# A 68-byte load on GpSimd, ahead of its constant fills, in an elementwise multiply-and-GELU kernel

## The chip, the core and the metric

The kernel runs on one core of one Trainium2 chip. The core has a vector engine (VectorE, DVE in the profile), a scalar engine (ScalarE, ACT), GpSimd (POOL), a tensor engine (PE, not used here) and SyncE (SP), which computes nothing and only waits and issues transfers. Transfers between the device memory and the core's on-chip memory (SBUF, 128 partitions) are carried out by 16 DMA engines that all issuing engines share. The metric is the device time of the program in microseconds, as the median of several executions.

## The reference

Two arrays of 1024 x 4096 float32 go in and one comes out. Each element is multiplied with its partner, and the product goes through the tanh form of GELU:

```python
z = x * y
return (0.5 * z * (1 + np.tanh(np.sqrt(2 / np.pi) * (z + 0.044715 * z ** 3)))).astype(np.float32)
```

There is no reuse of any element. 33.55 MB have to be read and 16.78 MB written.

## The kernel before

The 4,194,304 elements are seen as 128 partitions of 32,768 columns, cut into three pieces of columns: a small one of 1,280 columns (5 KB in each partition), one of 16,384 (64 KB) and one of 15,104 (59 KB). Each piece is contiguous in device memory, and within it each partition has one contiguous row. The buffer `xs` holds all of x on chip. The buffer `ys` holds only 20,440 columns, so the pieces of y share it: the 64 KB rows of y lie at columns 4,056 to 20,440 of `ys`, the 59 KB rows are written to columns 0 to 15,104 once VectorE has used the first part of the 64 KB rows, and the small piece comes last, to columns 15,104 to 16,384.

Six loads and three stores make up all the traffic. Two loads are issued ahead of everything: `_hoist` takes an issued instruction out of the place where it was written and puts it into the program's first block, ahead of that engine's first Drain, and so ahead of the barriers with which all engines start. SyncE so issues the small piece of x (`load_x(0)`, line 79), and ScalarE the 64 KB rows of x (`load_x(1)`, line 80). GpSimd in that first block fills four constants (memsets of one column each, put down to line 137) and then takes part in the start barriers. It does nothing after that.

The rest of the transfers is SyncE's queue, in this order: wait for the small piece of x (line 81), the 64 KB rows of y (line 82), the 59 KB rows of x (line 83), then, after VectorE's third multiply, the 59 KB rows of y, and after its fourth the small piece of y (lines 84 to 87). The stores follow (lines 112 to 116): the first one waits for the 59 KB rows of y to have landed and for ScalarE's fourth step, the others for ScalarE alone. Then SyncE waits for the stores, clears the semaphores and ends (lines 117 to 122).

VectorE multiplies in place (line 99) in 13 steps: four of 4,096 columns over the first pair of pieces, seven of 2,048 and one of 768 over the second, one of 1,280 over the last. ScalarE applies the GELU in place (line 107) to each step after VectorE. Semaphore `sem_mul` counts the multiplies, `sem_act` the activations, and each transfer has a semaphore of its own.

Of the kernel before, what the change touches and what calls it, by code (L numbers as in the profile page):

```python
# [1 line left out]

# [4 lines left out]


F32 = mybir.dt.float32
GELU = mybir.ActivationFunctionType.Gelu_apprx_tanh  # L10

PIECES = [(0, 1280), (1280, 17664), (17664, 32768)]

Y_LOADS = [(1280, 17664, 4056), (17664, 32768, 0), (0, 1280, 15104)]

Y_FREE = [0, 3, 4]

STEPS = [[4096] * 4, [2048] * 7 + [768], [1280]]  # L20
STORES = [(1280, 17664), (17664, 32768), (0, 1280)]
Y_BUF = 20440


def _hoist(nc, issued):

    here = nc.cur_bb.bb.instructions
    first = nc.main_func.blocks[0].instructions
    for ins in issued:
        del here[next(k for k, i in enumerate(here) if i is ins or i.name == ins.name)]  # L30
    engine = issued[0].engine
    at = next(
        k
        for k, i in enumerate(first)
        if i.engine == engine and type(i).__name__ == "InstDrain"
    )
    first[at:at] = issued


@with_exitstack  # L40
def kernel(
    ctx: ExitStack,
    tc: tile.TileContext,
    x: bass.AP,
    y: bass.AP,
    out: bass.AP,
):
    nc = tc.nc
    P = nc.NUM_PARTITIONS

    def columns(t, a, b):

        flat = t.flatten_outer_dims().rearrange("r c -> (r c)")
        pa, pb = next(q for q in PIECES if q[0] <= a and b <= q[1])
        return flat[P * pa : P * pb].rearrange("(p c) -> p c", p=P)[:, a - pa : b - pa]


    tc.close()
    tc.compile()

    xs = nc.alloc_sbuf_tensor("xs", [P, PIECES[-1][1]], F32).ap()
    ys = nc.alloc_sbuf_tensor("ys", [P, Y_BUF], F32).ap()
    sem_x = [nc.alloc_semaphore(f"sem_x{i}") for i in range(len(PIECES))]
    sem_y = [nc.alloc_semaphore(f"sem_y{i}") for i in range(len(Y_LOADS))]
    sem_mul = nc.alloc_semaphore("sem_mul")
    sem_act = nc.alloc_semaphore("sem_act")
    sem_o = [nc.alloc_semaphore(f"sem_o{i}") for i in range(len(STORES))]

    def load_x(i, engine=nc.sync):
        a, b = PIECES[i]  # L70
        return engine.dma_start(out=xs[:, a:b], in_=columns(x, a, b)).then_inc(sem_x[i], 16)

    def load_y(i):
        a, b, r = Y_LOADS[i]
        return nc.sync.dma_start(
            out=ys[:, r : r + b - a], in_=columns(y, a, b)
        ).then_inc(sem_y[i], 16)

    _hoist(nc, [load_x(0).ins])
    _hoist(nc, [load_x(1, nc.scalar).ins])  # L80
    nc.sync.wait_ge(sem_x[0], 16)
    load_y(0)
    load_x(2)
    for i in range(1, len(Y_LOADS)):
        if Y_FREE[i]:
            nc.sync.wait_ge(sem_mul, Y_FREE[i])
        load_y(i)

    nc.scalar.wait_ge(sem_x[0], 16)
    n = 0  # L90
    done = {}
    for i, (a, b, r) in enumerate(Y_LOADS):
        for j, (xa, xb) in enumerate(PIECES):
            if xa <= a < xb:
                nc.vector.wait_ge(sem_x[j], 16)
        nc.vector.wait_ge(sem_y[i], 16)  # L96
        c = a
        for w in STEPS[i]:
            nc.vector.tensor_mul(  # L99
                out=xs[:, c : c + w],  # L100
                in0=xs[:, c : c + w],
                in1=ys[:, r + c - a : r + c - a + w],
            ).then_inc(sem_mul, 1)
            n += 1
            done[c + w] = n
            nc.scalar.wait_ge(sem_mul, n)
            nc.scalar.activation(  # L107
                out=xs[:, c : c + w], in_=xs[:, c : c + w], func=GELU
            ).then_inc(sem_act, 1)
            c += w  # L110

    for i, (a, b) in enumerate(STORES):
        if i == 0:
            nc.sync.wait_ge(sem_y[-2], 16)
        nc.sync.wait_ge(sem_act, done[b])
        nc.sync.dma_start(out=columns(out, a, b), in_=xs[:, a:b]).then_inc(sem_o[i], 16)
    for i in range(len(STORES) - 1):
        nc.sync.wait_ge(sem_o[i], 16)
    nums = sorted(s.num for s in [*sem_x, *sem_y, *sem_o[:-1], sem_mul, sem_act])
    assert nums == list(range(nums[0], nums[-1] + 1))  # L120
    nc.sync.sem_clear(range(nums[0], nums[-1] + 1))
    nc.sync.wait_ge(sem_o[-1], 16).then_inc(sem_o[-1], -16)


# [1 line left out]
_INS = ['x', 'y']  # L126
_OUTS = [((1024, 4096), 'float32')]


# [23 lines left out]
```

## Time and profile before

| | value |
|---|---|
| median of 3 runs | 119.83 us (119.66 to 120.29) |
| profiled execution: span from the first instruction to the last | 118.5 us |
| profiled execution: a time of its own beside the span | none is given; the median of the runs is 1.3 us above the span |
| VectorE busy | 35.2 us (30%), 13 instructions |
| ScalarE busy | 30.9 us (26%), 14 instructions |
| GpSimd busy | 0.2 us, 4 instructions |
| bytes moved | 50.33 MB, 425 GB/s over the span |
| queue q1 (SyncE's transfers) | 41.94 MB |
| queue q10 (ScalarE's transfer) | 8.39 MB |

How to read it: instructions that only set registers, branch, wait, signal or issue a transfer are not counted as busy, so GpSimd's 0.2 us are its four constant fills alone. A row named SPq or ACTq is the issue of a transfer by SyncE or ScalarE; its duration is that of issuing, and the transfer's landing is given apart. The chain of work that ended last is followed back from the last instruction, and gives for each stretch what was being waited for.

### The profile page before, as it was taken

To read this page: it belongs to the slowest core of one execution; us is meant where nothing else is said; L and a number is where in the kernel's file an instruction comes from. 1 tells how busy PE (TensorE), PEld (TensorE's weight loads), DVE (VectorE), ACT (ScalarE), POOL (GpSimd) and SP (SyncE) were. 2 spreads that over 40 slices of the span, in tenths; PEclk is the share of its full clock that TensorE was granted. 3 is DMA by queue.
4 is the path that set the end of the run, shared out by engine and by line. 5 is a ranking of instruction groups with operands and counts; after the bars stand their busy time and mean duration, and the time that the engine had idled before them with its cause. 6 is when DMAs were issued, how large, how long until landed. Compare 5 with 4: busy or idle time off the path is not lost.

```text
span 118.5 us, 83 instructions
## 1 busy us (share of the span) xinstructions
DVE 35.2 (30%) x13; ACT 30.9 (26%) x14; POOL 0.2 (0%) x4
## 2 busy tenths in 40 slices
DVE  0000000000000069999920000059999940000000
ACT  0000000000000000999975000006998990000000
POOL 0000000000000000000000000000000000000000
DMA  9888899889988897798797797798899887977975
GB/s 492 382 382 382 354 597 464 354 354 465 597 354 354 354 632 347 326 632 347 326 632 347 326 632 347 326 575 354 354 531 531 354 354 326 653 326 326 653 326 221
DMA packets 1296, 50.33 MB, mean 425 GB/s; under 512 B 144, under 2 KB 144, under 8 KB 528
## 3 DMA queue, kind: packets, MB, share of 16 engines
q1 hardware_dynamic: 1152, 41.94, 82.3%
q10 hardware_dynamic: 144, 8.39, 16.5%
HBM read 33.55 MB, written 16.78 MB: 425 GB/s over the span
## 4 chain that ended last, share of the span: by engine, by line
DMA 55%; DVE 24%; ACT 3%; issue 1%; DVEq 0%
DMA ys<-in_y_dram 43%; DVE xs L99 24%; DMA xs<-in_x_dram 11%; ACT xs L107 3%; DVEq L96 0%
## 5 line engine op out<-in xcount | busy, mean ns | idle before, releaser
L99 DVE TENSOR_TENSOR xs<-xs,ys 128x2048 f32<-128x2048 f32 (+3 forms) x13 | 35.2, 2778 | 60.9 <-DMA ys<-in_y_dram 60.9
L107 ACT ACTIVATE xs<-xs 128x2048 f32<-128x2048 f32 (+3 forms) x13 | 29.6, 2300 | 19.6 <-DVE xs L99 19.6
L107 ACT ACT_TABLE_LOAD x1 | 1.3, 1283 | 47.2 <-DVE xs L99 47.2
L137 POOL MEMSET const-uint8-127<- 128x1 uint8 x1 | 0.1, 102 | 0.0
L137 POOL MEMSET const-bfloat16-1.0<- 128x1 bf16 x1 | 0.1, 101 | 0.0
L137 POOL MEMSET const-float32-0.0<- 128x1 f32 x1 | 0.1, 98 | 0.2 <-issue 0.2
L137 POOL MEMSET const-float32-1.0<- 128x1 f32 x1 | 0.1, 98 | 0.0
## 6 DMA issues: line engine op xcount, KB each, us to landing
xs<-in_x_dram SPq DMA_DIRECT2D x1, 7552.0 KB, 46.5
ys<-in_y_dram SPq DMA_DIRECT2D x1, 7552.0 KB, 22.5
out_dram<-xs SPq DMA_DIRECT2D x1, 7552.0 KB, 20.4
xs<-in_x_dram SPq DMA_DIRECT2D x1, 640.0 KB, 13.6
ys<-in_y_dram SPq DMA_DIRECT2D x1, 640.0 KB, 19.7
out_dram<-xs SPq DMA_DIRECT2D x1, 640.0 KB, 20.8
xs<-in_x_dram ACTq DMA_DIRECT2D x1, 30.4
ys<-in_y_dram SPq DMA_DIRECT2D x1, 29.0
```

The source lines that it names most:

```text
L99: nc.vector.tensor_mul(out=xs[:, c : c + w], in0=xs[:, c : c + w], in1=ys[:, r + c - a : r + c - a + w],).then_inc(sem_mul, 1)
L107: nc.scalar.activation(out=xs[:, c : c + w], in_=xs[:, c : c + w], func=GELU).then_inc(sem_act, 1)
L137: nc = _bacc.Bacc("TRN2", target_bir_lowering=False, num_devices=1)
```

## The change

GpSimd issues one more transfer: the first 17 elements of y (68 bytes, one contiguous stretch of the first row of its small piece) go to columns 0 to 17 of `ys` on partition 0. The data is not used: those columns are later overwritten by the 59 KB rows of y. The transfer signals a new semaphore, `sem_s`.

`_hoist` now also takes a Memset for the place to put an instruction in front of. SyncE's and ScalarE's hoisted loads stand where they stood, since those engines have no memset; GpSimd's new load comes ahead of its four constant fills, and is the first instruction of the kernel on that engine.

SyncE, ahead of the issue of y's 59 KB rows, waits for `sem_s` in addition to `sem_mul`, so that the 68 bytes can't land on top of them. The list of semaphores cleared at the end has one more in it. The order of all other instructions on every engine is as before.

```diff
+SPARE = 0
...
     at = next(
         k
         for k, i in enumerate(first)
-        if i.engine == engine and type(i).__name__ == "InstDrain"
+        if i.engine == engine and type(i).__name__ in ("InstDrain", "InstMemset")
     )
     first[at:at] = issued
...
+    sem_s = nc.alloc_semaphore("sem_s")
...
     _hoist(nc, [load_x(0).ins])
     _hoist(nc, [load_x(1, nc.scalar).ins])
+    spare = nc.gpsimd.dma_start(
+        out=ys[0:1, SPARE : SPARE + 17], in_=columns(y, 0, 17)[0:1, :]
+    ).then_inc(sem_s, 16)
+    _hoist(nc, [spare.ins])
     nc.sync.wait_ge(sem_x[0], 16)
     load_y(0)
     load_x(2)
     for i in range(1, len(Y_LOADS)):
         if Y_FREE[i]:
             nc.sync.wait_ge(sem_mul, Y_FREE[i])
+        if i == 1:
+            nc.sync.wait_ge(sem_s, 16)
         load_y(i)
...
-    nums = sorted(s.num for s in [*sem_x, *sem_y, *sem_o[:-1], sem_mul, sem_act])
+    nums = sorted(s.num for s in [*sem_x, *sem_y, *sem_o[:-1], sem_s, sem_mul, sem_act])
```

## The prediction

> **What bounds the kernel now.** I read the page first, then the chain of waits, then the timeline of the start, then what SyncE's queue waits for, and last a table of stretches.
>
> From the page, the engines, the traffic and the issues:
>
> ```profile
> span 118.5 us, 83 instructions
> DVE 35.2 (30%) x13; ACT 30.9 (26%) x14; POOL 0.2 (0%) x4
> ...
> HBM read 33.55 MB, written 16.78 MB: 425 GB/s over the span
> ...
> xs<-in_x_dram SPq DMA_DIRECT2D x1, 640.0 KB, 13.6
> ys<-in_y_dram SPq DMA_DIRECT2D x1, 640.0 KB, 19.7
> ```
>
> No engine is busy for a third of the span, and the DMA engines carry 425 GB/s from end to end. The last two lines are x's small piece, landing 13.6 us after its issue, and y's small piece, 19.7 us.
>
> The chain that ended last, in order of time, its first pieces:
>
> ```profile
> 0.00 13.56 DMA xs<-in_x_dram
> 13.56 0.02 issue
> 13.57 28.99 DMA ys<-in_y_dram
> ...
> 42.66 13.11 DVE xs L99 x3
> 55.77 0.02 issue
> 55.79 22.46 DMA ys<-in_y_dram
> ```
>
> The chain names VectorE between 42.66 and 55.77, but the transfers do not pause there, as the table of stretches below shows: x's 59 KB rows are still coming. So the bound is the byte count, and an instruction costs time only if it leaves the DMA engines without work.
>
> The timeline of the first 14 us (start, duration, what):
>
> ```profile
> 0.00 0.38 SPq L71 DMA_DIRECT2D xs<-in_x_dram  x1
> 0.12 0.36 ACTq L71 DMA_DIRECT2D xs<-in_x_dram  x1
> 0.23 0.10 POOL L137 MEMSET const-float32-0.0<- 128x1 f32 x1 [0.23 <-issue]
> ...
> 13.57 0.33 SPq L75 DMA_DIRECT2D ys<-in_y_dram  x1
> ```
>
> Only two transfers are issued before 13.57 us, neither by GpSimd. GpSimd's fills begin at 0.23 us and are the first work of any kind that counts as busy; the next is VectorE's multiply at 42.66.
>
> SyncE's own waits:
>
> ```profile
> SPq L75 <- DVE xs L99: 45.4, 2, 41.4
> ...
> SPq L75 <- DMA xs<-in_x_dram: 12.1, 1, 12.1
> ```
>
> SyncE waits 12.1 us for x's small piece and 41.4 us for the third multiply: room in front of both of its steps that the change touches.
>
> Stretches of the span (length, busy times, granted clock, DMA share, GB/s):
>
> ```profile
> 0.00:1.00 1.00, 0.00 (x0) 0.00 (x0) 0.20 (x4) 1.00 0.00 0
> 1.00:2.00 1.00, 0.00 (x0) 0.00 (x0) 0.00 (x0) 1.00 0.98 276
> ...
> 3.00:13.50 10.50, 0.00 (x0) 0.00 (x0) 0.00 (x0) 1.00 0.98 423
> ...
> 42.50:55.80 13.30, 13.14 (x4) 8.41 (x4) 0.00 (x0) 1.00 1.01 436
> 55.80:60.40 4.60, 4.30 (x1) 3.88 (x2) 0.00 (x0) 1.00 0.97 420
> 60.40:78.20 17.80, 0.00 (x0) 3.35 (x1) 0.00 (x0) 1.00 0.92 400
> ```
>
> Nothing moves in the first microsecond; from then on the share is close to 1. (A packet's bytes are booked at its start, hence the ups and downs.) The reader is to see that only the first microsecond is free of traffic.
>
> **The change, part by part.** The sum is made against the profiled span of 118.5 us, and the median of the runs, 119.83, is 1.3 us above it. What those 1.3 us are, and where the time starts and ends against the span, no row shows.
>
> *The bytes.* The load is one row of 68 bytes on one partition. The nearest row is y's small piece, 128 rows of 5 KB. The last issue of a load of y starts at 60.1, and this one lands 19.7 us later, at 79.8; the 59 KB rows ahead of it land at 55.79 + 22.46 = 78.25. So its 8 rows for each DMA engine take 1.56 us, 0.2 us for one. A 68-byte row takes between 0 and 0.2 us, on one engine of sixteen; I take 0.05, nearer to nothing, because it has a 75th of the bytes. This lies straight on the path if that engine is the slowest, since the DMA engines are never idle: +0.05 us.
>
> *The completion on each engine.* Each transfer also signals. From x's 59 KB rows (landed 13.96 + 46.5 = 60.46) to y's (78.25) 17.8 us pass for eight rows, 2.22 us for a row of 59 KB, with a transfer's end in between; at the 436 GB/s of the stretch from 42.5 to 55.8, 7.73 MB take 17.7 us. So a hand-over costs at most 0.1 us. I put it in with the 0.05.
>
> *GpSimd's issue.* This engine has issued no transfer before, so its price is not in the trace. The nearest rows are the issues on SyncE and ScalarE, 0.33 to 0.43 us (the two of 0.38 and 0.36 at the start). The other end is that GpSimd holds its next instruction until the data is there: the nearest row is then x's small piece, landing 13.6 us after its issue, in the same crowd. Between these stands the time from the first issue to the first moving byte, 1.0 us (no traffic in the stretch 0 to 1). I take 1.0, because an issuing engine has to have handed its transfer over by then, and the load is far smaller than the piece that lands at 13.6. Behind it on GpSimd's queue are the four memsets, which then begin at about 1.2 us instead of 0.23, its Drain, and its part in the start barriers. All other engines wait for that barrier, so it releases them about 1 us later. None of them needs it: SyncE's next issue waits for x's small piece until 13.57, VectorE's first multiply is at 42.66, ScalarE's table load at 47.17. The barriers have to be later than 13.57 us to show at all; the two early loads are ahead of the barrier and are not held. Cost on the transfers: nothing, up to a delay of some 12 us. If the cover were gone, each further microsecond would hold y's 64 KB rows back, though x's 64 KB rows, on the wire until 0.12 + 30.4 = 30.5 us, would still feed the engines for a while. The Trainium skill (DMA: Bandwidth & Descriptors, "SWDGE vs HWDGE vs iDMA") says that a transfer issued by GpSimd has its descriptors computed by software on that engine, where SyncE's come from hardware, and the same page's "Specifications" have about 1 µs to the first byte for the one and 0.6 for the other; no run here shows GpSimd's. By the ratio of those, an estimate, the issue would be 1.7 times SyncE's 0.38, 0.6 us, in place of the 1.0 above, and the forecast below would be 0.4 us higher.
>
> *SyncE's wait for `sem_s`.* It stands in front of the issue at 55.79; behind it are y's 59 KB rows, y's small piece and all stores. The load, issued before 0.3 us, lands at the latest like x's small piece, after some 14 us, so the wait finds it done with 41 us to spare. The instruction itself may take 0.02 us, the size of the chain's issue pieces. That too is covered: x's 59 KB rows keep the DMA engines at work until 60.4, 4.6 us past the issue. Without that cover it would be 0.02 us. The one semaphore more that is cleared at the end lies in a single range instruction: nothing.
>
> *Where the time starts.* Everything above leaves the span at 118.5 to 118.6. What has no cover is the start of the count. The time is not the span: 119.83 against 118.5, so it has ends of its own. The profile does not count issuing, waiting and signalling as work, and by that account the program's first work is GpSimd's memset at 0.23. If the time runs from there, and not from SyncE's issue at 0.00, then holding the memsets back by 1.0 us while the two early loads run takes 1.0 us off: between 0.36 (a hardware issue) and 13.6 (held until landing). The end does not move.
>
> Sum: 119.83 - 1.0 + 0.05 = 118.9 us, rounded to 118.8 because a dispatch ahead of the issue (GpSimd's fills start 0.1 us after ScalarE's first instruction) adds about 0.1 to the delay.
>
> **The rivals.**
>
> *The start is not moved.* If the time is counted from the first instruction of any kind, SyncE's issue at 0.00, then nothing is saved, and the 0.05 to 0.15 us of extra traffic remain: 119.9 us. For it speaks that the span is counted so. Against it nothing in the profile speaks; it is only that the time and the span differ. The change then does nothing measurable, since all its waits are covered. The Trainium skill (same page, "Issuing engines are not separate DMA queues") says that transfers of all issuing engines run on the same 16 DMA engines and interleave, which is what the rows of q1 and q10 show: that speaks for this rival, and moves no number.
>
> *A turn of a third queue.* Slower: the load goes through a queue that the kernel doesn't use yet, and every DMA engine has to turn to it once, while x's two first pieces come in and no engine has slack. The place is the stretch from 1 to 13.5 us. The price is at most one turn of a 64 KB row per engine: 2.22 us x 64/59 = 2.4 us, if an engine stands still while it fetches and completes the odd transfer; at least the 0.05 above. It decides from 0.6 us. The middle is 1.2 us, so 119.83 + 1.2 = 121.0, and 122.2 at most. For it: the engines are saturated, so what is lost there isn't won back. Against it: q1 and q10 take turns from 3 to 13.5 us at 423 GB/s, within 3% of the 436 of a stretch with q1 alone. The Trainium skill (same page, "Latency and other measured facts") reports the rings of GpSimd's transfers as its best guess for why two of the 16 DMA engines run slower; no run here shows it, and with a single 68-byte transfer it would act only in this stretch.
>
> *GpSimd is held for long.* If the issue held GpSimd past 13.57 us, the barrier would hold y's 64 KB rows. The landing of x's small piece, 13.6 us, is the far bound, so at most a fraction of a microsecond would be lost on the path. I give it no more than 0.02, within the slower case.
>
> **How the numbers follow.** The start moved: 0.48, 116.8 to 119.5 with 118.8 in the middle; the start not moved: 0.27, 119.8 to 120.0; the third queue's turn or a held barrier: 0.25, 120.4 to 122.2. I give the first most because it is the only part of the change that no other work covers; I do not give it more because no row shows where the count starts. The likeliest gives 118.8. About 0.5%, 0.6 us, is what a measurement of this kernel can tell from no change: the three runs differ by that much. The first case falls under 119.23 nearly always, so faster 0.48, same 0.27, slower 0.25. The range: from 117.2, a delay of 2.6 us (one turn of a 64 KB row and one of 5 KB, 2.4 + 0.2), which leaves out some 0.04 below, to 120.7, which takes in all of the second case and the smaller third of the third, leaving out some 0.16 above. The likeliest case's own range is 117.2 to 119.5.
>
> **What the changed profile would show.** The bytes: 50.33 MB still, a third queue with hardly any share, and landings of the nine transfers within 0.2 us of 13.6, 42.6, 60.4, 78.2, 79.8 and 118.5. GpSimd's issue: a row on GpSimd ahead of the memsets, and the first memset at about 1.2 us; if it is at 0.3, the issue costs nothing and the delay is wrong. The wait: SyncE's issue of y's 59 KB rows at about 55.8, still put down to VectorE. The start: a span that is the same while the runs' time falls is the first case; both the same is the second; landings of x's and y's first pieces later by 0.6 us or more is the third. The prediction is wrong if the time is counted from SyncE's first issue, or if the DMA engines lose a turn.

## The result, and the profile after

The changed kernel takes 119.27 us (median of 4 runs, 119.15 to 119.36) against 119.85 us, a ratio of 0.9954 with a 95% interval of 0.9936 to 0.9972. A second comparison, with more runs of the kernel before, gave 119.28 us and 0.9949 (0.9937 to 0.9961). So 0.58 us are gone, beyond doubt, and right at the 0.5% that the prediction had named as the least that can be told from no change.

The page of the changed kernel: its span, the new queue, GpSimd's rows and its new issue (the last column of the last line is the time to landing).

```profile
span 118.5 us, 85 instructions
DVE 35.2 (30%) x13; ACT 30.9 (26%) x14; POOL 0.8 (1%) x5
...
q0 software_dynamic: 32, 0.00, 0.0%
...
L83 POOL DMA_DIRECT2D ys<-in_y_dram x1 | 0.6, 632 | 0.7 <-issue 0.7
...
L145 POOL MEMSET const-float32-0.0<- 128x1 f32 x1 | 0.1, 128 | 0.0
...
ys<-in_y_dram POOLq DMA_DIRECT2D x1, 0.1 KB, 10.0
```

The span is 118.5 us, as before. The run that this profile was taken in took 119.36 us, so 0.8 us lie around the span (118.53 us to two places) where there had been 1.3. And the load stands among the rows that count as busy: GpSimd has five of them now, 0.8 us in place of 0.2. The issues of SyncE and ScalarE have no such row.

The timeline of its start:

```profile
0.00 0.39 SPq L73 DMA_DIRECT2D xs<-in_x_dram  x1
0.12 0.36 ACTq L73 DMA_DIRECT2D xs<-in_x_dram  x1
0.74 0.63 POOL L83 DMA_DIRECT2D ys<-in_y_dram  x1 [0.74 <-issue]
1.35 0.13 POOL L145 MEMSET const-float32-0.0<- 128x1 f32 x1
```

The fills begin at 1.35 us instead of 0.23, but the load itself begins at 0.74. GpSimd's first work is 0.51 us later than before, not 1.1.

The chain, its first pieces and those around 55.8:

```profile
0.00 15.99 DMA xs<-in_x_dram
15.99 0.02 issue
16.01 26.57 DMA ys<-in_y_dram
42.58 0.03 issue
...
55.80 22.46 DMA ys<-in_y_dram
```

x's small piece landed at 16.0 in this execution, not at 13.6, and y's 64 KB rows were issued 2.4 us later. They still landed at 42.6, as before. The experiments show the same shift in a kernel without the load.

What SyncE waited for: the start barrier in the kernel before, then two lines of the changed kernel:

```profile
SPq L137 <- PEq L137: 0.3, 1, 0.3
```

```profile
SPq L145 <- PEq L145: 10.5, 1, 10.5
SPq L77 <- DMA xs<-in_x_dram: 4.3, 1, 4.3
```

The start barrier, 0.3 us long before, holds SyncE for 10.5 us. The engine named is only another one that takes part; the trace has GpSimd's Drain ahead of that barrier at 10.0 us, where it had been 0.18. It begins at 0.81 us and ends at 10.8, just after the load has landed, at 0.74 + 10.0 = 10.7 us.

### The profile page after: what moved, and what is told of

Read it like the earlier page. It is cut to its first block, busy times and chain, and to the rows that moved or that the text cites. A ratio compares the mean times of both kernels' runs of the same rounds, so it can differ in the third digit from the quotient of the medians.

```text
span 118.5 us, 85 instructions
## 1 busy us (share of the span) xinstructions
DVE 35.2 (30%) x13; ACT 30.9 (26%) x14; POOL 0.8 (1%) x5
## 4 chain that ended last, share of the span: by engine, by line
DMA 55%; DVE 24%; ACT 3%; issue 1%; DVEq 0%
DMA ys<-in_y_dram 41%; DVE xs L107 24%; DMA xs<-in_x_dram 13%; ACT xs L115 3%; DVEq L104 0%
## 5 line engine op out<-in xcount | busy, mean ns | idle before, releaser
L83 POOL DMA_DIRECT2D ys<-in_y_dram x1 | 0.6, 632 | 0.7 <-issue 0.7
```

Source lines behind the costliest of these rows:

```text
L83: spare = nc.gpsimd.dma_start(out=ys[0:1, SPARE : SPARE + 17], in_=columns(y, 0, 17)[0:1, :]).then_inc(sem_s, 16)
```

## The experiments

Three theories stood against each other. Theory S: the time starts with the first work, which the change moves, and the end stays where it is. Theory T: the gain comes from what the load does to the first transfers. And within S, two forms: only the fills count as first work (as the prediction's sum had it), or the load counts itself. Each edit is shown against the changed kernel, except where the text names another.

**The load behind the fills**

```diff
-        if i.engine == engine and type(i).__name__ in ("InstDrain", "InstMemset")
+        if i.engine == engine and type(i).__name__ == "InstDrain"
```

> The same load of 68 bytes on GpSimd, but issued behind its four constant fills. Theory S (the time starts at GpSimd's first work, a fill or the load itself, and its end does not move): the fills are back at 0.23 us, so nothing is saved: 119.85 us, ratio 1.000, at most 0.1 us off. Theory T (the gain comes from what the load does to the first transfers): the load is still there, x's small piece still lands at about 16 us, and the time is 119.3, ratio 0.995.

Measured: 119.77 us, ratio 0.9997 (0.9989 to 1.0006). The timeline:

```profile
0.24 0.09 POOL L145 MEMSET const-float32-0.0<- 128x1 f32 x1 [0.24 <-issue]
...
0.84 0.63 POOL L83 DMA_DIRECT2D ys<-in_y_dram  x1 [0.40 <-issue]
13.39 0.33 SPq L77 DMA_DIRECT2D ys<-in_y_dram  x1
```

The same load, 0.1 us later, and the gain is gone: what matters between these two is what stands first on GpSimd. The start barrier is as late as in the changed kernel (SyncE waits 10.4 us for it), so neither the load's traffic nor the late barrier makes a difference to the time. That x's small piece landed at 13.4 us with the load present is not what this expectation had said; see below.

**No load, the fills wait**

```diff
+    _hoist(nc, [nc.gpsimd.wait_ge(sem_x[0], 16).ins])
     nc.sync.wait_ge(sem_x[0], 16)
     load_y(0)
```

(This edit is to the kernel before. `_hoist` puts the wait ahead of the fills, by the same choice of place as in the changed kernel.)

> No added load; GpSimd's constant fills wait for x's small piece, which lands at about 13.6 us. Theory S: the first work begins at 13.6 instead of 0.23 us, the last store still ends at about 118.5 us of the span, and the time falls by 13.4 us, to about 106.5. Theory T: without the load there is nothing to gain, and a later start barrier (about 14.1 us) costs nothing or a little: 119.85 to 120.5. In both the span stays at 118.5 us.

Measured: 106.50 us, ratio 0.8892 (0.888 to 0.8904). The head of its page, then its timeline:

```profile
span 118.5 us, 83 instructions
```

```profile
0.00 0.38 SPq L71 DMA_DIRECT2D xs<-in_x_dram  x1
...
13.48 0.10 POOL L138 MEMSET const-float32-0.0<- 128x1 f32 x1 [13.48 <-DMA xs<-in_x_dram]
...
14.62 0.33 SPq L75 DMA_DIRECT2D ys<-in_y_dram  x1
```

Theory S had said 106.5, theory T 119.85 or more. The program runs as long as ever, from SyncE's first issue to its last instruction 118.5 us, and 13.3 us of it are no longer in the time, with no load at all.

**The load on SyncE**

```diff
-    spare = nc.gpsimd.dma_start(
+    spare = nc.sync.dma_start(
```

> The same 68 bytes, issued by SyncE behind x's small piece in place of GpSimd; GpSimd has only its four fills. Theory S: the fills begin at 0.23 us as before, so the time is 119.85 us, ratio 1.000, at most 0.1 us off. Theory T in the form that any small load early helps: 119.3, ratio 0.995. It also tells whether GpSimd's Drain of 10 us and the later landing of x's small piece (16.0 against 13.6 us) come from the load as such or from its being issued by GpSimd: with SyncE issuing, no long Drain, and a landing at 13.6 to 13.8.

Measured: 119.74 us, ratio 0.9998 (0.9989 to 1.0007). SyncE's waits and the landing of x's small piece:

```profile
SPq L77 <- DMA xs<-in_x_dram: 11.8, 1, 11.8
SPq L94 <- DMA ys<-in_y_dram: 3.6, 1, 3.6
...
SPq L145 <- PEq L145: 0.2, 1, 0.2
```

```profile
xs<-in_x_dram SPq DMA_DIRECT2D x1, 640.0 KB, 13.6
```

An early load of 68 bytes, issued by SyncE, gains nothing. As a test of theory T this is weaker than the first experiment, because the data moves late here: in the trace the packet of 68 bytes begins at 15.2 us, after x's small piece has landed, where it began at 4.7 us in the first experiment. It lands at 18.0 us: SyncE, through with its issues at 14.4, waits another 3.6 us for it (the line L94). The long start barrier is gone. On SyncE the load lands long after the barrier has ended; on GpSimd the barrier ended only once the load had landed.

**The fills wait for the load**

```diff
     _hoist(nc, [spare.ins])
+    _hoist(nc, [nc.gpsimd.wait_ge(sem_s, 16).ins])
```

> The changed kernel, with GpSimd's fills waiting until the 68 bytes have landed (about 10.7 us). Theory S with the load itself counted as first work, at 0.74 us: the time is that of the changed kernel, 119.27, ratio 0.995. Theory S in the form of the prediction (only the fills count): the first fill is at 10.8 us and the time falls to 109.3. Theory T: the traffic is that of the changed kernel, 119.27.

Measured: 119.35 us, ratio 0.9961 (0.9946 to 0.9977). The timeline:

```profile
0.74 0.63 POOL L83 DMA_DIRECT2D ys<-in_y_dram  x1 [0.74 <-issue]
10.84 0.10 POOL L146 MEMSET const-float32-0.0<- 128x1 f32 x1 [9.47 <-DMA ys<-in_y_dram]
```

The first fill is at 10.8 us and the time has not fallen any further. So the load is itself the first work, and only its own start counts. This is the term that the prediction mis-sized.

**The fills wait, and VectorE starts early**

```diff
+    _hoist(nc, [nc.gpsimd.wait_ge(sem_x[0], 16).ins])
+    _hoist(nc, [nc.vector.memset(ys[:, 0:1], 0.0).ins])
```

(To the kernel before, with the place chosen as in the changed kernel.)

> GpSimd's fills wait for x's small piece as in the kernel that took 106.5 us; in addition VectorE fills one column of ys as its first instruction, ahead of its Drain. Theory S with the first work of any engine as the start: VectorE's fill at about 0.15 us starts the time, and it is back at 119.9 us (118.5 of the span, less 0.15, plus the 1.56 us that lay around it so far). Rival, the start is tied to GpSimd alone: 106.5 us again. Rival, later fills shorten something real in the run: 106.5 us again.

Measured: 120.00 us, ratio 1.0007 (0.9997 to 1.0016). The timeline:

```profile
0.15 0.06 DVE L82 MEMSET ys<- 128x1 f32 x1
15.88 0.10 POOL L139 MEMSET const-float32-0.0<- 128x1 f32 x1 [15.88 <-DMA xs<-in_x_dram]
```

One VectorE instruction of 0.06 us brings back the 13 us that the waiting fills had taken off. The start belongs to the first work of any engine, not to GpSimd.

This execution settles another point. There is no 68-byte load in this kernel, and x's small piece lands at 15.8 us.

**The changed kernel again**

> The changed kernel itself once more, against the kernel before on one chip, for a closer ratio. Theory S: the start moved from 0.23 to 0.74 us, 0.51 us of 119.8, ratio 0.9957. The prediction's size, a delay of 1.0 us, would be a ratio of 0.991. It also tells whether x's small piece again lands at 16.0 us and not at 13.6.

Measured: 119.28 us, ratio 0.9949, as given above. Its interval, 0.9937 to 0.9961, takes in the 0.9957 of theory S and leaves out the 0.991. In this profile x's small piece landed at 13.5 us:

```profile
0.00 13.52 DMA xs<-in_x_dram
13.54 29.02 DMA ys<-in_y_dram
```

The same kernel has had it at 16.0 and at 13.5, and a kernel without the load at 15.8. The two landings differ by one turn of a 64 KB row (2.4 us), and in the trace of each late one x's 64 KB rows begin after 64 packets of the small piece, four for each of the 16 DMA engines, in the others after 80, five for each. In both late profiles with GpSimd's load its first packet begins at 4.6 us, and x's 64 KB rows had begun at 2.0 and 2.1, so the load's packets did not set that order. Late were two of the four profiles with GpSimd's load and one of the five without, too few to tell whether its issue makes it more frequent. What decides between the two was not tried; the time is the same with either.

**The fills wait for x's 64 KB rows**

```diff
-    _hoist(nc, [nc.gpsimd.wait_ge(sem_x[0], 16).ins])
+    _hoist(nc, [nc.gpsimd.wait_ge(sem_x[1], 16).ins])
```

(Against the kernel of "No load, the fills wait".)

> GpSimd's fills wait for x's 64 KB rows, so the start barrier holds back SyncE's issue of y's 64 KB rows until these have landed, at about 22.3 us with nothing beside them. The cover is gone: the issue comes at about 23.4 us, its first bytes at about 25.4 (2 us after, as in the kernel before), and the DMA engines stand idle for some 3 us, so the span grows from 118.5 to about 121.9 us. Theory S: the time is nevertheless span - 22.3 + 1.56 = 101.2 us, a shorter time for a run that ends later. Rival, the time falls only by as much as the run really gets shorter: 121 to 123 us.

Measured: 100.51 us, ratio 0.8383 (0.8371 to 0.8394). The head of its page; its timeline; and its stretches from 20 to 26 us (length, busy times, granted clock, DMA share, GB/s):

```profile
span 122.0 us, 83 instructions
```

```profile
23.17 0.10 POOL L138 MEMSET const-float32-0.0<- 128x1 f32 x1 [23.17 <-DMA xs<-in_x_dram]
...
24.31 0.33 SPq L75 DMA_DIRECT2D ys<-in_y_dram  x1
```

```profile
20.00:21.00 1.00, 0.00 (x0) 0.00 (x0) 0.00 (x0) 1.00 1.06 459
21.00:22.00 1.00, 0.00 (x0) 0.00 (x0) 0.00 (x0) 1.00 0.00 0
...
24.00:25.00 1.00, 0.00 (x0) 0.00 (x0) 0.00 (x0) 1.00 0.00 0
25.00:26.00 1.00, 0.00 (x0) 0.00 (x0) 0.00 (x0) 1.00 2.73 918
```

Here the barrier is late enough to hurt. The last of x's 64 KB rows begin before 21 us, no further row begins until 25, and the program ends 3.5 us later than before. The time is nevertheless shorter by 19 us. The expected 101.2 was 0.7 us too high, since x's rows landed at 23.1 us and not at 22.3.

**One sum for all of them.** From the traces: the start of the first work, the span, the profiled run's own time, and what is left when the span is taken off and the start is added.

| kernel | first work, us | span, us | time, us | time - span + first work |
|---|---|---|---|---|
| before | fill, 0.23 | 118.52 | 119.83 (median) | 1.54 |
| changed | load, 0.74 | 118.53 | 119.36 | 1.57 |
| load behind fills | fill, 0.24 | 118.38 | 119.70 | 1.56 |
| fills wait, no load | fill, 13.48 | 118.52 | 106.61 | 1.57 |
| load on SyncE | fill, 0.23 | 118.57 | 119.90 | 1.56 |
| fills wait for load | load, 0.74 | 118.58 | 119.40 | 1.56 |
| fills wait, VectorE fill | VectorE's fill, 0.15 | 118.85 | 120.27 | 1.57 |
| changed, again | load, 0.73 | 118.51 | 119.34 | 1.56 |
| fills wait for x's 64 KB rows | fill, 23.17 | 122.05 | 100.44 | 1.56 |

Over starts from 0.15 to 23 us and spans from 118.4 to 122.0 us the remainder is 1.56 to 1.57 us in each profiled run. So the time is the span, less what passes before the first work, plus 1.56 us. Whether these lie behind the program's last instruction or in part ahead of the first work, no row shows. SyncE's and ScalarE's issues of transfers, though they start the data moving, do not start the time; GpSimd's does.

## Why the prediction came out as it did

**The direction and the place** were right: the start of the time moved, and its end did not. The span is unchanged, and an added load without a later start gains nothing (0.9997 and 0.9998).

**The size** was not. The step *GpSimd's issue* took a delay of 1.0 us, on the footing that the time would start at the first fill. The fill did move by 1.12 us (0.23 to 1.35). But the load is itself work by the profile's account, which the prediction had not considered: it looked at the rows for issues on SyncE and ScalarE and took over that issues don't count. What counts is the load's start, 0.74 - 0.23 = 0.51 us, of the 0.58 measured (the rest is within the spread of the runs). The prediction had this part as well, but only as the 0.1 us of dispatch ahead of the issue; the 1.0 us that it put on the issue itself does not count. That its 1.0 and 0.1 come near the fill's 1.12 is chance: those are 0.51 us ahead of the issue and 0.61 from the issue's start to the first fill. With the load's start in its place the sum is 119.83 - 0.51 + 0 = 119.32, against 119.27. That is inside the likeliest case's range, 117.2 to 119.5, though just above the 119.23 under which the prediction looked for this case nearly always. The estimate that the prediction made from the Trainium skill (DMA: Bandwidth & Descriptors, "Specifications"), an issue of 0.6 us, agrees with the row: 0.63 us on GpSimd against 0.39 on SyncE. The page's two figures are for the first byte, though, and not for the issue; here the load's first packet begins at 4.6 us, among the 64 KB rows. The issue, too, stands behind the load's start and so does not enter the time.

**The barrier** was expected to be released about 1 us later, with the load's landing as the far bound. It came with the landing, as in the far bound, but not by the way named there: GpSimd's next instructions, the fills, were not held and began at 1.35 us; the Drain waited for the landing, and SyncE was held for 10.5 us. The cover named for it, SyncE's wait for x's small piece until 13.57, was there, and it was good for more: in the kernel without a load the barrier came at 14.5 us, y's 64 KB rows were issued at 14.62, 1.05 us later than before, and still landed at 42.5. Where the cover was really gone, with the issue at 24.31, the program lost 3.5 us.

**The bytes and the completion**, 0.05 us, cannot be told from nothing: the spans are 118.4 to 118.6 us with the load, and 118.5, 118.5 and 118.9 without it, the kernel with idle DMA engines left out. **The wait for `sem_s`** found the load landed 45 us earlier; y's 59 KB rows were issued at 55.80 as against 55.79.

**The rivals.** *The start is not moved* fell with the 106.5 us run. *A turn of a third queue* fell with the first experiment: the queue is there, with 32 packets, and the time is that of before. Its sign in the profile, x's small piece landing more than 0.6 us late, did appear, and would have misled: it was there once without the load and absent twice with it on GpSimd, and y's 64 KB rows behind it land at 42.4 to 42.6 us either way. *GpSimd is held for long*: GpSimd was held until 10.8 us, by its Drain and not by the issue. That is short of the 13.57 us that this rival needed, and it cost nothing.

## What to carry to other kernels

Before a gain is put down to the work, ask whether the end of the work has moved. Here the last store lands when it did before; the 0.58 us came from the start of the count, and one experiment shortened the time by 16% while the program ended 3.5 us later, so neither the changed kernel nor those with waiting fills is faster at its work. Where the time and the span differ, take the difference apart over several kernels: a remainder that stays the same to 0.01 us is worth more than an argument. And in the kernels here a transfer on GpSimd ahead of the start barrier held that barrier until it had landed; the same transfer on SyncE did not.

## What the runs showed of the hardware that was not expected

- GpSimd's Drain behind a transfer of 68 bytes took 10.0 us, until that transfer landed in the crowd of 64 KB rows. With the same transfer on SyncE the start barrier took 0.2 us, though that transfer landed only at 18.0 us.
- The transfer from GpSimd made 32 packets, of which one carries the 68 bytes and took 12 ns, the others 4 bytes each.
- GpSimd's issue begins only at 0.74 us, though the engine's first instruction is at 0.14; behind the fills it begins 0.40 us after they end.
- x's small piece, unchanged in all the kernels, landed at 13.4 to 13.6 us in some executions and at 15.8 to 16.0 in others, with no effect on the time. What decides stays open.
